# Mixers: the weights' sums and lower halves all on POOL, VectorE without them

## The chip, the cores and the metric

The kernel runs on one core of a Trainium2 chip. The metric is the device time of one execution in microseconds (us). The engines are PE (TensorE), DVE (VectorE), ACT (ScalarE), POOL (GpSimd) and SP, which here issues nearly all DMAs. Each engine works through its own list of instructions in order; the lists are fixed when the kernel is built, and engines wait for one another by semaphores.

## What is computed

One layer of an encoder, for 1,024 prompt tokens and 64 tokens of a running stream: a SwiGLU half step, then differential softmax attention and retention side by side (the mixers), merged by sigmoid gates, then a second SwiGLU half step and a norm. All in float32. The mixers begin with one wide projection:

```python
hm = modulate(rms_norm(x, norm_mix), shm, scm)
q_a, k_a, v_a, q_r, k_r, v_r, z_r, gate_a, gate_r = jnp.split(hm @ w_in, offsets, axis=-1)   # 1024 x 5120
o_a = diff_attention_prompt(q_a, k_a, v_a, lam)      # 4 heads, and one over a cache of 2048 for the stream
o_r, s_new = retention_prompt(q_r, k_r, v_r, log_g)  # 4 heads, states carried over blocks
```

## The kernel before

Three stages follow one another: the first SwiGLU, the mixers, then the merge and the second SwiGLU. The tokens are worked on in two groups, g = 0 (512 tokens) and g = 1 (576). The change concerns the mixers alone, where the wide projection of `w_in` is done 128 columns by 128.

**Split products.** A float32 factor is split into an upper half `hi` (a rounded copy, made by ACT, line 134) and a lower half `lo = x - hi` (line 138, on an engine that is handed in). `mm3` (lines 162 to 164) multiplies hi by hi, hi by lo and lo by hi, so each product of a 128-row slice is three matmuls, and the third needs the weights' lower half.

**Pairs.** Two blocks of 128 columns make a pair. `pair_weights` loads both (512 KB each, tiles `raw`: a1, a2 and b1, b2 are their halves) and forms Strassen-like sums (line 521): s1 = b1 + b2, s2 = s1 - a1, s3 = a1 - b1, s4 = a2 - s2. Four tiles are split: `ra` itself (call its halves wa), the tile of s1 and s2 (ws), the tile of s3 and s4 (wt), and b2 (wb, half as wide). `products` then makes 7 products of 12 matmuls from them, in this order: wa, ws, ws, wa, wt, wt, wb. In the mixers the tile of s1 and s2 is a slot called `h15` and that of s3 and s4 is `h14`. There are 20 pairs for each group, 40 in all; the weights of the first are made in the stage before, so 39 are made in the mixers.

**Buffers.** `whi` and `wlo` have 3 buffers each, so wa, ws and wt of a pair take the place of wa, ws and wt of the pair before, and each may be written only when its last product there has been done. `wb` has one buffer: it is free after the last product of the pair before.

**Who does what** is set by two lists for each stage. `LOE` names the engine for the lower halves of wa, ws, wt, wb and, fifth, of the down weights (not used in the mixers); `SE` names the engine for s1, s2, s3, s4. `phase(1)` puts the second row of `LOES` and `SES` in force for the mixers. `V` is `nc.vector` (DVE), `G` is `nc.gpsimd` (POOL).

**Around it.** Between the products, generators put in the attention (scores line 1067, row maximum 1071, exponential 1073, its coefficient 1079 and difference 1080 on DVE, values 1090), the rotation of retention (1207 to 1209, DVE), its norm (874 on DVE, then a power on POOL, 875), and the sums of the second group's activations (383 to 416, mostly DVE, one in four sums on POOL). DVE also reads every product out of PSUM and adds it up (line 521, `t`, `ft` and `u` with `misc` as an input, 128x256 or 128x288). When the group changes, the split activations of the next group are written (line 138, `h<-u,h`): five of seven on DVE, two on POOL. A scheduler with a timeline of its own sets the final order of each engine's list when the kernel is built, so a change of engines also moves instructions that it does not touch.

Of the kernel before, what the change touches and what calls it, by code (L numbers as in the profile page):

```python
# [83 lines left out]
def encoder_layer(tc: tile.TileContext, a, o, stage=9):  # L84
# [80 lines left out]

    V, G = nc.vector, nc.gpsimd
    LOE, SE = [], []
    LOES = [[G, V, V, V, G], [G, V, G, V, V], [G, V, V, G, G]]
    SES = [[G, G, G, G], [G, V, G, G], [V, V, G, G]]
    FE = [[V, V, G, G], [G, G, G, G], [V, V, V, G], [V, V, G, G]]  # L170

    def phase(i):
        LOE[:], SE[:] = LOES[i], SES[i]

# [1397 lines left out]
```

## Time and profile before

| | us |
|---|---|
| median of 3 runs | 2621.68 (2621.64 to 2623.53) |
| the profiled execution | 2621.47 |
| its span in the trace | 2619.7 |
| busy in the span: PE, DVE, POOL, ACT | 2479.6, 1992.8, 1621.9, 1079.0 |

The pairs made in the mixers start their first product at 883.8 us of the span, and the last pair's last product ends at 1606.6. In the trace matmuls are pipelined. A row of a group gives busy time, mean time of one, and the idle time of the engine ahead of it with what ended it. "Granted clock" 1.00 is 2.4 GHz, 0.50 is 1.2 GHz.

### The profile page before, as it was taken

What the parts mean: (1) busy time and instruction counts of PE and PEld (TensorE: products, weight loads), DVE (VectorE), ACT (ScalarE), POOL (GpSimd) and SP (SyncE); (2) the same over time, 40 slices, a digit from 0 to 9 for tenths busy, and PEclk for the clock granted to TensorE, in tenths of its full rate; (3) what the DMA queues carried; (4) which work ended last, traced back from release to release, by engine and by line L of the source; (5) the groups of instructions that cost most, each with busy time, mean ns of one, the idle gap of its engine ahead of it and who ended that gap; (6) DMA issues with size and microseconds to landing.
All of it is one profiled execution on the core that took longest, in us unless ns stands there. A gap on an engine that the chain in (4) does not pass through costs nothing. (4 is left out here: it accounts for less than half of the span.)

```text
span 2619.7 us, 45289 instructions
## 1 busy us (share of the span) xinstructions
PE 2479.6 (95%) x17278; PEld 2273.4 (87%) x17278; DVE 1992.8 (76%) x3241; ACT 1079.0 (41%) x1726; POOL 1621.9 (62%) x970
## 2 busy tenths in 40 slices
PE   6999999999999689998999999999999999999998
PEld 3888888999999678887888887798889998999998
DVE  6797778887767888788765675646898888877776
ACT  4443334443333333444434444533444435333333
POOL 4797677787665546667454543554777665766562
PEclk9999999999999899998999999999899999999999
DMA  8755446444443553444333335745443335323221
GB/s 276 222 181 161 150 141 209 144 151 137 152 133 107 180 173 111 155 134 131 109 101 106 118 103 160 232 138 182 149 152 117 105 106 180 104 89 97 90 87 40
DMA packets 427309, 367.60 MB, mean 140 GB/s; under 512 B 20060, under 2 KB 359700, under 8 KB 427092
## 3 DMA queue, kind: packets, MB, share of 16 engines
q1 hardware_dynamic: 426912, 364.65, 44.7%
q8 instruction: 136, 2.23, 0.3%
q14 instruction: 81, 0.66, 0.1%
q10 hardware_dynamic: 180, 0.06, 0.0%
HBM read 310.31 MB, written 52.10 MB: 138 GB/s over the span
## 5 line engine op out<-in xcount | busy, mean ns | idle before, releaser
L162 PE MATMUL misc<-h,whi 128*128 128x288 f32 (+2 forms) x3360 | 1012.2, 302 | 40.5 <-DVE t L521 21.9
L164 PE MATMUL misc<-h,wlo 128*128 128x288 f32 (+2 forms) x3360 | 986.2, 295 | 12.5 <-DVE wlo L138 11.5
L163 PE MATMUL misc<-h,whi 128*128 128x288 f32 (+2 forms) x3360 | 989.6, 295 | 5.0 <-DVE h L138 5.0
L162 PEld LDWEIGHTS misc<-h,whi 128*128 128x128 f32 x3360 | 645.5, 192 | 91.7 <-DVE t L521 25.1
L164 PEld LDWEIGHTS misc<-h,wlo 128*128 128x128 f32 x3360 | 644.8, 192 | 21.5 <-DVE wlo L138 13.5
L163 PEld LDWEIGHTS misc<-h,whi 128*128 128x128 f32 x3360 | 646.1, 192 | 13.9 <-DVE h L138 6.6
L138 POOL TENSOR_TENSOR wlo<-raw,whi 128x1024 fp32r<-128x1024 f32 x150 | 374.4, 2496 | 215.7 <-ACT whi L134 191.6
L521 DVE TENSOR_TENSOR t<-misc,t 128x256 f32<-128x256 f32 (+1 forms) x736 | 307.5, 432 | 252.8 <-PE misc L164 223.5
L138 DVE TENSOR_TENSOR wlo<-ws,whi 128x1024 fp32r<-128x1024 f32 x178 | 327.2, 1839 | 70.7 <-ACT whi L134 70.7
L138 POOL TENSOR_TENSOR wd<-raw,wd 128x1024 fp32r<-128x1024 f32 x88 | 210.8, 2415 | 142.1 <-ACT wd L134 142.1
L521 POOL TENSOR_TENSOR ws<-raw 128x512 f32<-128x512 f32 x134 | 194.2, 1452 | 117.8 <-DVE wlo L138 75.9
L643 DVE SCALAR_TENSOR_TENSOR x<-misc,gate,x 128x64 f32<-128x64 f32 (+3 forms) x540 | 237.1, 484 | 20.1 <-PE misc L164 19.4
L134 ACT CAST whi<-ws 128x1024 fp32r<-128x1024 f32 x178 | 186.5, 1048 | 159.6 <-PE misc L163 94.4
L134 ACT CAST whi<-raw 128x1024 fp32r<-128x1024 f32 x160 | 167.4, 1046 | 196.4 <-PE misc L163 157.3
L521 DVE TENSOR_TENSOR v<-t 128x288 f32<-128x288 f32 (+1 forms) x176 | 184.6, 1060 | 2.5 <-ACT t L604 2.3
L162 PE MATMUL misc<-h,wd 128*128 128x288 f32 (+3 forms) x552 | 178.1, 329 | 2.4 <-DVE t L521 1.6
L163 PE MATMUL misc<-h,wd 128*128 128x288 f32 (+3 forms) x552 | 179.8, 326 | 0.0
L164 PE MATMUL misc<-h,wd 128*128 128x288 f32 (+3 forms) x552 | 178.5, 326 | 0.0
L521 POOL TENSOR_TENSOR h<-raw 128x512 f32<-128x512 f32 x78 | 111.3, 1427 | 86.0 <-issue 39.1
L134 ACT CAST wd<-raw 128x1024 fp32r<-128x1024 f32 x88 | 88.3, 1047 | 170.4 <-PE misc L163 150.8
L162 PE MATMUL misc<-h,wb 128*128 128x256 f32 (+1 forms) x512 | 151.6, 296 | 1.9 <-ACT t L588 1.7
L163 PE MATMUL misc<-h,wb 128*128 128x256 f32 (+1 forms) x512 | 149.0, 291 | 0.0
(294 smaller groups left out, 4911.2 us busy)
## 6 DMA issues: line engine op xcount, KB each, us to landing
raw<-in_w_up_dram SPq DMA_DIRECT2D x176, 512.0 KB, 4.0
raw<-in_w_down_dram SPq DMA_DIRECT2D x88, 512.0 KB, 3.5
raw<-in_w_in_dram SPq DMA_DIRECT2D x80, 512.0 KB, 4.0
rawa<-in_w_ada_dram SPq DMA_DIRECT2D x88, 256.0 KB, 4.3
yf<-xsp SPq DMA_DIRECT2D x32, 288.0 KB, 4.2
h<-in_w_ada_dram SPq DMA_DIRECT2D x16, 512.0 KB, 6.8
raw<-in_w_o_dram SPq DMA_DIRECT2D x16, 512.0 KB, 4.7
raw<-far SPq DMA_DIRECT2D x14, 576.0 KB, 3.8
```

Source lines behind the costliest of these rows:

```text
L134: nc.scalar.copy(hi, src)
L138: eng.tensor_tensor(out=lo, in0=src, in1=hi.bitcast(F32), op=ALU.subtract)
L162: nc.tensor.matmul(out, wh, xh, start=first, stop=False)
L163: nc.tensor.matmul(out, wh, xl, start=False, stop=False)
L164: nc.tensor.matmul(out, wl, xh, start=False, stop=last)
L521: eng.tensor_tensor(out=out, in0=in0, in1=in1, op=op)
L643: nc.vector.scalar_tensor_tensor(out=xm, in0=t[:, c0 - cs.start:c1 - cs.start], scalar=gate()[:, m, s:s + 1], in1=xm, op0=ALU.mult, op1=AL ...
```

## The change

Two rows of the tables are other ones. In the mixers s2, the lower half of ws and the lower half of wb go from DVE to POOL, which then makes all four sums and all four lower halves of every pair.

```diff
-    LOES = [[G, V, V, V, G], [G, V, G, V, V], [G, V, V, G, G]]
-    SES = [[G, G, G, G], [G, V, G, G], [V, V, G, G]]
+    LOES = [[G, V, V, V, G], [G, G, G, G, V], [G, V, V, G, G]]
+    SES = [[G, G, G, G], [G, G, G, G], [V, V, G, G]]
```

Over the 39 pairs this moves 117 instructions from DVE's list to POOL's. What it does to the lists is shown where the first group's pairs are closest together (near 1180 us of the span). POOL before, from s1 of a pair (weights raw_13677 and raw_13678) to the lower half of its wt, with two instructions of its neighbours in between; h15 and h14 are the sums' tiles, raw the loaded weights, in brackets what an instruction waits for:

```order
L521 TENSOR_TENSOR h15_13681<-raw_13678 128x512 [waits DMAHW2_49,DVE_49,Pool_49]
L138 TENSOR_TENSOR wlo_13556<-h14_13542,whi_13555 128x1024 [waits PE_49,Activation_49]
L521 TENSOR_TENSOR h14_13682<-raw_13677,raw_13678 128x512 [waits DMAHW5_49,Pool_49]
L521 TENSOR_TENSOR h14_13682<-raw_13677,h15_13681 128x512 [waits DVE_49]
L138 TENSOR_TENSOR wlo_13684<-raw_13677,whi_13683 128x1024 [waits PE_49,Activation_49]
L521 TENSOR_TENSOR h15_13887<-raw_13884 128x512 [waits DMAHW7_49,DVE_49,Pool_49]
L138 TENSOR_TENSOR wlo_13696<-h14_13682,whi_13695 128x1024 [waits PE_49,Activation_49]
```

POOL now, for the same pair:

```order
L521 TENSOR_TENSOR h15_13681<-raw_13678 128x512 [waits DMAHW1_49,Pool_49]
L138 TENSOR_TENSOR wlo_13684<-raw_13677,whi_13683 128x1024 [waits DMAHW2_49,PE_49,Activation_49]
L521 TENSOR_TENSOR h14_13682<-raw_13677,raw_13678 128x512 [waits Pool_49]
L521 TENSOR_TENSOR h15_13681<-h15_13681,raw_13677 128x512 [waits Pool_49]
L138 TENSOR_TENSOR wb_13700<-raw_13678,wb_13699 128x512 [waits PE_49,Activation_49]
L521 TENSOR_TENSOR h14_13682<-raw_13677,h15_13681 128x512 [waits Pool_49]
L138 TENSOR_TENSOR wlo_13690<-h15_13681,whi_13689 128x1024 [waits Activation_49]
L138 TENSOR_TENSOR wlo_13696<-h14_13682,whi_13695 128x1024 [waits PE_49,Activation_49]
```

The lower half of ws (wlo_13690) now stands last but one of the eight, behind the one of wb, which waits for the last product of the pair before. DVE before, in the same pair:

```order
L521 TENSOR_TENSOR h15_13681<-h15_13681,raw_13677 128x512 [waits DMAHW5_49,Pool_49]
L521 TENSOR_TENSOR ft_13385<-misc_13519,t_13413 128x256 [waits DVE_49,PE_49]
L138 TENSOR_TENSOR wb_13560<-raw_13538,wb_13559 128x512 [waits DMAHW4_49,Activation_49]
L521 TENSOR_TENSOR t_13564<-misc_13580,t_13563 128x256 [waits DVE_49,PE_49,Activation_49]
L521 TENSOR_TENSOR t_13565<-misc_13594,t_13564 128x256 [waits DVE_49,PE_49]
L521 TENSOR_TENSOR ft_13535<-misc_13616,t_13563 128x256 [waits DMAHW1_49,PE_49]
L138 TENSOR_TENSOR wlo_13690<-h15_13681,whi_13689 128x1024 [waits Activation_49]
```

DVE now, at the same products:

```order
L521 TENSOR_TENSOR ft_13385<-misc_13519,t_13413 128x256 [waits DVE_49]
L521 TENSOR_TENSOR ft_13384<-misc_13500,t_13414 128x256 [waits PE_49]
L521 TENSOR_TENSOR ft_13535<-misc_13616,t_13563 128x256 [waits DMAHW0_49,PE_49,Activation_49]
L521 TENSOR_TENSOR t_13564<-misc_13580,t_13563 128x256 [waits DVE_49,PE_49]
L521 TENSOR_TENSOR t_13565<-misc_13594,t_13564 128x256 [waits DVE_49,PE_49]
```

Only the readings of products out of PSUM are left. PE's list moves with it; now, at the second and third product of such a pair (misc_13580 and misc_13594, weights ws):

```order
L162 MATMUL misc_13580<-h2_9708,whi_13549 128x256 [waits DVE_49,Activation_49]
L163 MATMUL misc_13580<-h3_9709,whi_13549 128x256
L162 MATMUL misc_13594<-h4_9716,whi_13549 128x256 [waits DVE_49]
L163 MATMUL misc_13594<-h5_9717,whi_13549 128x256
L1047 MATMUL misc_13609<-ident_66,rows_13133 128x128 [waits DVE_49]
```

Before, all 24 matmuls of the two products stood there in one run; now only the four that need no lower half do, and the others stand behind the fourth product and the first matmuls of the fifth and sixth.

## Rows read from the trace of the kernel before

**Rows 1.** The page's first part: busy us of each engine, share, instructions.

```profile
PE 2479.6 (95%) x17278; PEld 2273.4 (87%) x17278; DVE 1992.8 (76%) x3241; ACT 1079.0 (41%) x1726; POOL 1621.9 (62%) x970
```

**Rows 2.** Windows of the mixers: length, PE, PEld, DVE, ACT, POOL busy; granted clock; DMA.

```profile
883.80:1013.80 130.00, 101.82 (x673) 89.88 (x672) 109.00 (x215) 49.33 (x96) 69.60 (x47) 0.87 0.51 152
1013.80:1060.70 46.90, 46.90 (x348) 40.63 (x346) 37.66 (x89) 23.01 (x50) 33.29 (x20) 1.00 0.35 107
1060.70:1196.90 136.20, 131.34 (x995) 120.19 (x995) 113.41 (x202) 64.79 (x129) 95.25 (x57) 0.99 0.49 156
1196.90:1235.90 39.00, 28.91 (x183) 27.34 (x182) 32.48 (x40) 12.98 (x22) 25.12 (x14) 0.82 0.38 116
1235.90:1606.60 370.70, 365.92 (x2472) 311.98 (x2470) 251.61 (x481) 155.96 (x282) 177.02 (x117) 1.00 0.35 105
```

**Rows 3.** Groups of DVE in the mixers (883.8 to 1606.6), shapes apart.

```profile
L138 DVE TENSOR_TENSOR wlo<-h,whi 128x1024 fp32r<-128x1024 f32 x39 | 54.9, 1408 | 9.3 <-ACT whi L134 9.3
L521 DVE TENSOR_TENSOR h<-h,raw 128x512 f32<-128x512 f32 x38 | 53.7, 1412 | 5.6 <-POOL h L521 5.3
L138 DVE TENSOR_TENSOR wb<-raw,wb 128x512 fp32r<-128x512 f32 x39 | 45.9, 1177 | 3.1 <-ACT wb L134 2.4
```

**Rows 4.** Sums and lower halves in the mixers: ns min/median/max, first and last start.

```profile
L521 POOL TENSOR_TENSOR h<-raw x76: 1257/1300/2424, 887.5 to 1563.1; 128x512 f32<-128x512 f32 x76
...
L138 POOL TENSOR_TENSOR wlo<-h,whi x39: 2352/2397/2912, 888.7 to 1582.8; 128x1024 fp32r<-128x1024 f32 x39
L521 DVE TENSOR_TENSOR h<-h,raw x38: 657/693/2889, 891.5 to 1558.6; 128x512 f32<-128x512 f32 x38
```

**Rows 5.** The lower half of wb on POOL, in the second SwiGLU (same columns).

```profile
L138 POOL TENSOR_TENSOR wb<-raw,wb x44: 1262/1759/2270, 1830.0 to 2570.5; 128x512 fp32r<-128x512 f32 x44
```

**Rows 6.** Order of time, 895 to 920: start, us, engine, operation, [idle before].

```profile
896.03 0.28 PE L163 MATMUL misc<-h,whi 128*128 128x256 f32 x1
...
896.15 0.28 PE L164 MATMUL misc<-h,wlo 128*128 128x256 f32 x1
...
905.06 2.86 POOL L138 TENSOR_TENSOR wlo<-h,whi 128x1024 fp32r<-128x1024 f32 x1
...
906.09 1.84 DVE L1079 SCALAR_TENSOR_TENSOR col<-col,lam 128x1 f32<-128x1 f32 x1
...
908.56 0.73 DVE L388 TENSOR_TENSOR sqf<-sqf,yf 128x576 f32<-128x576 f32 x1
...
910.29 1.64 PE L1067 MATMUL S<-u 64*128 64x384 f32 x2 [6.73 <-ACT c L1073]
```

**Rows 7.** Groups of DVE, 883.8 to 1013.8.

```profile
L388 DVE TENSOR_TENSOR sqf<-sqf,yf 128x576 f32<-128x576 f32 x7 | 11.9, 1693 | 2.2 <-ACT yf L386 2.1
L521 DVE TENSOR_TENSOR h<-h,raw 128x512 f32<-128x512 f32 x7 | 9.8, 1402 | 0.5 <-POOL h L521 0.3
...
L138 DVE TENSOR_TENSOR wlo<-h,whi 128x1024 fp32r<-128x1024 f32 x7 | 8.5, 1216 | 1.6 <-ACT whi L134 1.6
...
L138 DVE TENSOR_TENSOR wb<-raw,wb 128x512 fp32r<-128x512 f32 x6 | 5.9, 991 | 0.0
```

**Rows 8.** Groups of POOL, 1060.7 to 1196.9, shapes apart.

```profile
L521 POOL TENSOR_TENSOR h<-raw 128x512 f32<-128x512 f32 x19 | 27.0, 1419 | 13.5 <-DVE wlo L138 2.7 <-PE misc L163 2.5 <-PE misc L164 2.4
L138 POOL TENSOR_TENSOR wlo<-raw,whi 128x1024 fp32r<-128x1024 f32 x10 | 24.8, 2476 | 15.8 <-ACT whi L134 15.8
L138 POOL TENSOR_TENSOR wlo<-h,whi 128x1024 fp32r<-128x1024 f32 x9 | 22.7, 2524 | 0.9 <-ACT whi L134 0.9
L521 POOL TENSOR_TENSOR h<-raw,h 128x512 f32<-128x512 f32 x10 | 15.2, 1521 | 0.6 <-DVE h L521 0.6
```

**Rows 9.** Waits of POOL, 1060.7 to 1196.9.

```profile
POOL col L875 <- DVE col L874: 9.9, 3, 4.8
```

**Rows 10.** A stretch of the first SwiGLU, columns as in the second group.

```profile
150.00:200.00 50.00, 48.74 (x354) 43.89 (x352) 44.98 (x56) 21.62 (x33) 46.13 (x28) 1.00 0.61 195
```

**Rows 11.** Groups of DVE at the change of group, 1196.9 to 1235.9.

```profile
L138 DVE TENSOR_TENSOR h<-u,h 128x576 fp32r<-128x576 f32 x7 | 13.2, 1913 | 0.0
```

## The prediction

> **What bounds the kernel now.** The page's first part comes first: PE is busy for 95% of the span and DVE for 76%, POOL for 62% [rows 1]. The change touches only the mixers, so the windows of the mixers come next, cut at the starts of pairs [rows 2]; in each the reader compares the stretch's length with PE, DVE and POOL.
>
> - 883.8 to 1013.8 (130.0 us, 6 pairs): PE busy 101.8, so idle 28.2, at a mean granted clock of 0.87. DVE is the fullest of the feeders at 109.0, POOL has 69.6.
> - 1013.8 to 1196.9 (46.9 + 136.2 = 183.1 us, 13 pairs): PE busy 178.2, clock near 1.00. DVE 151.1, POOL 128.5. Here PE bounds and neither feeder does.
> - 1196.9 to 1235.9 (39.0 us, the change of group): PE idle 10.1; DVE 32.5, POOL 25.1.
> - 1235.9 to 1606.6 (370.7 us): PE idle 4.8. POOL 177.0. PE bounds.
>
> So PE is idle for 38 us in the first and third of these stretches, and for 10 in the other 554. The longest single wait in the first is 6.73 us, on an exponential of the attention, and the order of time shows what was late behind it: DVE, which at 906.09 needs 1.84 us for a 128x1 operation that begins inside a 2.86 us lower half on POOL and ends with it [rows 6].
>
> That is a pattern. DVE's operations with two inputs in SBUF stretch when POOL runs: s2 takes 657 ns at best, 2889 at worst [rows 4], and its mean in the mixers is 1412 [rows 3].
>
> **What the change removes from DVE.** In the mixers the three kinds of moved instruction cost DVE 54.9 + 53.7 + 45.9 = 154.5 us [rows 3] over 39 pairs, 4.0 a pair (the first s2 starts ahead of the window).
>
> **What it adds to POOL.** A sum takes 1.30 us, a lower half of 128x1024 2.40 (medians, [rows 4]). The half-width lower half doesn't occur on POOL in the mixers; in the second SwiGLU it takes 1.26 at its shortest and 1.76 in the median [rows 5]. I take 1.3, near the shortest, since the DVE work that stretched it is what leaves. So 1.30 + 2.40 + 1.30 = 5.0 us a pair. A pair's own POOL work becomes 4 x 1.30 + 3 x 2.40 + 1.30 = 13.7 us, where its 84 matmuls, one every 0.12 us at full clock [rows 6], take 10, and the 13 pairs of the dense stretch follow one another at 183.1 / 13 = 14.1.
>
> Stretch by stretch, against the profiled execution's own time of 2621.47 us (span 2619.7 and 1.8 around it; the median of the runs is 0.2 above).
>
> *Dense stretch, 183.1 us.* POOL: 128.5 + 13 x 5.0 = 193.5. Its present instructions get shorter when DVE's rivals go: 19 x (1.419 - 1.30) + 10 x (1.521 - 1.30) + 10 x (2.476 - 2.40) + 9 x (2.524 - 2.40) = 6.3 us over 10 pairs [rows 8], so 8.2 over 13. That leaves 185.3 us in 183.1: POOL would have to work without a pause. It can't. It still waits for DVE's column ahead of the power of the norms (9.9 us over 10 pairs now, [rows 9]), and each lower half waits for a buffer that PE frees. With the fullest window that I read, 46.13 of 50 us or 92% [rows 10], the stretch needs 185.3 / 0.92 = 201.4, which is 18 more; without any pause it needs 2 more. I take +13, nearer the upper end: 185.3 plus the 9.9 us of that wait, and a microsecond for the buffers, is 196. What is queued behind: in the new order the lower half of ws stands behind that of wb, which waits for the last product of the pair before. After that product come 0.6 (the cast) + 1.3 + 1.3 (s4) + 2.4 = 5.6 us until ws is there, while PE has the rest of the fifth and sixth products (22 x 0.12), the first of the next (12) and the fourth (12) to do, 46 x 0.12 = 5.5. That fits alone, but leaves no room for a POOL that is already behind.
>
> *Start, 130.0 us.* DVE loses 9.8 + 8.5 + 5.9 = 24.2 us [rows 7]. POOL rises from 69.6 by 6 x 5.0 to about 100, from 54% to 77% of the stretch, so DVE's other operations with two SBUF inputs meet it more often: the 7 squares' sums average 1.69 us here [rows 7] where one takes 0.73 at its shortest [rows 6], so 6.7 us of theirs is waiting, and I estimate 10 more for the rotation and the far sums. If these 17 us grow as POOL's share does (77/54), 7 come back. Net DVE relief is 17 us. How much of it was on PE's path? PE is idle for 28.2 of 130 us, but the other 102 are PE's own, a part at the lower clock. I take half, -8. Bounds: 0, and -24 (all of it, without new contention).
>
> *Change of group, 39.0 us.* DVE loses 2 x 4.0 = 8 us and keeps 13.2 of activations that must be split [rows 11]. POOL rises from 25.1 by 2 x 5.0 to 35 of 39, and starts with what it is behind from the dense stretch. I take +3, between -6 (DVE was the late one) and +9 (POOL is late by its 10 new us, less one).
>
> *Rest, 370.7 us.* POOL 177.0 + 18 x 5.0 = 267, 72%: it has room, PE is the bound and can give back at most its 4.8 idle us. 0, from -3 to +5.
>
> *Everything else* stays: both SwiGLU stages and the merge use other rows of the tables, and what comes ahead of the mixers keeps its order. DMA count and sizes are the same.
>
> Sum: -8 + 13 + 3 + 0 = +8, so 2621.5 + 8 = **2629.5 us**.
>
> **A page that speaks against the change.** DVE's small operation was held to the end of POOL's [rows 6]. The Trainium skill, "Perfetto Trace Analysis", section "Optimizing Scalar/DVE Operations", says that GpSimd and VectorE share an SBUF read port, so that offloading between those two might not help. By that rule alone the result is rival B. And the Trainium skill, "SBUF — State Buffer", section "Who interferes with whom", says that a VectorE instruction with at most one SBUF input doesn't contend with GpSimd: by that the PSUM readings left in DVE's list run freely and rival C gains. The trace so far agrees with the second on the two-input operations.
>
> **Rivals.**
>
> A (the forecast): POOL becomes the bound where pairs are dense. For it: 185 us of work in 183. Against it: lower halves are made some microseconds ahead of need, so that a short excess is swallowed.
>
> B: it evens out. Start -11, dense +9, change of group +2, rest 0: 2621.5. For it: the terms are of one size and opposite sign.
>
> C: DVE's relief decides, faster. The place is the start: the full net relief of 17 us reaches PE, and 1 more come back through the clock, since short waits there go with 0.87. Dense +4, since POOL's 185 us run with next to no pause once DVE's column comes early, and the change of group -4. That is -18: 2603.5. It decides when POOL keeps busy for 99% of the dense stretch (185.3 in 183.1 + 4); at the 95% that +13 stands for, A wins.
>
> D: the change doesn't do what it says. The new lists show all 117 instructions on POOL, so I give it nothing.
>
> **How the numbers follow.** What a measurement of this kernel can tell from no change is about 0.2%, 5.2 us, so "same" is 2616.4 to 2626.9. A has 0.50, B 0.22, C 0.28. A's own range is 2627 to 2648 (start 0, dense 18, change of group 9 gives 2648.5). The range leaves out a little of C's far end and of A's: 2606 to 2648.
>
> **What would show it.** A: in the 13 dense pairs POOL's share above 90%, and PE with new waits on a lower half from POOL (line 164, weights ws). C: PE's idle time of the first 6 pairs under 14 us, DVE there under 95 busy, clock above 0.92. Contention: the two-input operations that stay on DVE (1079, 1080, 1207, 388) get longer, not shorter, while POOL's sums fall to about 1.3 us. I am wrong if the dense stretch doesn't get longer than 187 us, or if PE waits for POOL after 1236 us too.

## The result, and the profile after

The changed kernel takes 2640.31 us (median; 2635.75 to 2641.66), the kernel before 2621.66: a ratio of 1.0075, 95% interval 1.0057 to 1.0092. It is slower by 18.6 us. Direction and range hold; the predicted 2629.5 is 10.8 us short, so that the rise is more than twice the 8 us forecast. All figures below are of fast runs: one of the five runs of e2_but_one took 3407.58 us at a mean granted clock of 0.65 and is left out. The profiled execution after took 2635.75 us (span 2633.9), 14.3 more than the profiled one before.

The page's first part of the kernel after, to be laid beside [rows 1]:

```profile
PE 2483.1 (94%) x17278; PEld 2276.9 (86%) x17278; DVE 1883.1 (71%) x3124; ACT 1079.3 (41%) x1726; POOL 1800.7 (68%) x1087
```

DVE has 117 instructions and 110 us fewer, POOL 117 more and 179 us more, PE 3.5 us more. The windows of the mixers, cut at the starts of the same pairs as in [rows 2] (columns: length; busy us of PE, PEld, DVE, ACT, POOL; granted clock; share of the DMA engines; GB/s):

```profile
890.30:1023.00 132.70, 102.72 (x674) 91.47 (x674) 100.11 (x198) 50.18 (x99) 100.58 (x65) 0.86 0.50 151
1023.00:1069.10 46.10, 46.10 (x347) 40.31 (x346) 28.04 (x77) 22.00 (x48) 42.38 (x28) 1.00 0.38 114
1069.10:1215.30 146.20, 134.44 (x993) 122.97 (x992) 79.70 (x176) 64.25 (x129) 136.76 (x85) 0.96 0.47 145
1215.30:1255.80 40.50, 30.55 (x187) 27.77 (x187) 23.09 (x36) 13.95 (x23) 39.49 (x25) 0.87 0.33 99
1255.80:1628.50 372.70, 364.91 (x2473) 312.15 (x2473) 211.42 (x426) 155.38 (x281) 260.96 (x171) 0.99 0.35 106
```

The start is 2.7 us longer than before, the dense pairs 46.1 + 146.2 = 192.3 against 183.1, the change of group 1.5 longer. In the dense pairs POOL is busy for 42.38 + 136.76 = 179.1 us, 93%, where it was 70%; DVE fell from 151 to 108 there. Of TensorE's waits from 880 to 1650 us these stand out (engine, tile, line, what it waited for: us in all, times, longest):

```profile
PE misc L162 <- ACT whi L134: 14.8, 7, 6.7
PE misc L162 <- DVE t L521: 12.3, 6, 5.2
PE misc L1282 <- DVE s L1272: 8.4, 3, 6.7
```

The first is new: the cast on ACT ends the wait. What was late behind the cast differs by place. In the change of group (9.0 us of the 14.8, most of it in two waits of 6.75 and 2.02) it is POOL: each of the two casts had itself waited 5.17 us for one of POOL's sums. The first of them, in order of time on POOL, ACT and PE (start, us, engine, operation, [idle before and what ended it]):

```profile
1220.82 1.77 POOL L521 TENSOR_TENSOR h<-h,raw 128x512 f32<-128x512 f32 x1
...
1222.63 1.04 ACT L134 CAST whi<-h 128x1024 fp32r<-128x1024 f32 x1 [5.17 <-POOL h L521]
...
1223.72 0.61 PE L162 MATMUL misc<-h,whi 128*128 128x288 f32 x1 [6.75 <-ACT whi L134]
```

In the dense pairs (four waits, 5.8 us, all in the last three pairs) POOL's sum was ready 1.4 to 5.4 us before the cast began. There the cast stood in ACT's list behind other work that waits for PE, three times behind the copy of the same pair's first product out of PSUM (line 895):

```profile
1186.96 1.30 POOL L521 TENSOR_TENSOR h<-h,raw 128x512 f32<-128x512 f32 x1
...
1189.67 0.37 ACT L895 COPY t<-misc 128x256 f32<-128x256 f32 x1 [3.33 <-PE misc L164]
...
1189.94 1.05 ACT L134 CAST whi<-h 128x1024 fp32r<-128x1024 f32 x1
...
1191.04 0.39 PE L162 MATMUL misc<-h,whi 128*128 128x256 f32 x1 [1.45 <-ACT whi L134]
```

In the kernel before, the cast of a dense pair's sum tile begins 5.9 to 12.4 us ahead of that copy. After, it is 1.5 to 9.6 us ahead of it in the first ten dense pairs, where four casts start as soon as POOL's sum ends, and 0.3 to 1.4 us behind it in the last three. The time goes the same way: the copies are 8.8 us later than in the kernel before at the first dense pair (1024.3 against 1015.5) and 7.1 at the tenth (1157.1 against 1150.0). So the stretch's loss is made in its last pairs, when the lead is used up.

The longest wait of PE in the dense pairs, 4.05 us, is of another kind. A read-out of PSUM by DVE (`ft`) stood behind line 1080, which took 2.80 us beside POOL's lower halves; the mean of that shape was 0.96 us before:

```profile
1158.02 4.71 POOL L138 TENSOR_TENSOR wlo<-h,whi 128x1024 fp32r<-128x1024 f32 x2
...
1160.48 2.80 DVE L1080 SCALAR_TENSOR_TENSOR c<-c,col,c 128x512 f32<-128x512 f32 x1
...
1163.76 0.55 PE L162 MATMUL misc<-h,whi 128*128 128x256 f32 x1 [4.05 <-DVE ft L521]
```

The kinds of instruction of [rows 3] are gone from DVE; they stand on POOL now, with its own, where these are the largest groups (mixers; busy us, mean ns of one, idle before):

```profile
L138 POOL TENSOR_TENSOR wlo<-h,whi 128x1024 fp32r<-128x1024 f32 x78 | 189.7, 2436 | 48.4 <-ACT whi L134 45.2 <-PE misc L1150 2.0 <-PE misc L164 1.0
L521 POOL TENSOR_TENSOR h<-raw 128x512 f32<-128x512 f32 x76 | 105.2, 1391 | 0.9
...
L138 POOL TENSOR_TENSOR wb<-raw,wb 128x512 fp32r<-128x512 f32 x39 | 51.7, 1326 | 12.8 <-ACT wb L134 12.7
L521 POOL TENSOR_TENSOR h<-h,raw 128x512 f32<-128x512 f32 x38 | 51.4, 1353 | 0.9
```

### The profile page after: what moved, and what is told of

It is laid out like the page before. It is cut to its first block, busy times and chain, and to the rows that moved or that the text cites. A ratio compares the mean times of both kernels' runs of the same rounds, so it can differ in the third digit from the quotient of the medians.

```text
span 2633.9 us, 45291 instructions
## 1 busy us (share of the span) xinstructions
PE 2483.1 (94%) x17278; PEld 2276.9 (86%) x17278; DVE 1883.1 (71%) x3124; ACT 1079.3 (41%) x1726; POOL 1800.7 (68%) x1087
## 5 line engine op out<-in xcount | busy, mean ns | idle before, releaser
L164 PE MATMUL misc<-h,wlo 128*128 128x288 f32 (+2 forms) x3360 | 985.8, 296 | 11.3 <-DVE wlo L138 10.3
L138 POOL TENSOR_TENSOR wlo<-h,whi 128x1024 fp32r<-128x1024 f32 x78 | 189.7, 2436 | 48.4 <-ACT whi L134 45.2
L138 POOL TENSOR_TENSOR wb<-raw,wb 128x512 fp32r<-128x512 f32 x83 | 126.7, 1527 | 124.1 <-ACT wb L134 117.8
L162 PE MATMUL misc<-h,wb 128*128 128x256 f32 (+1 forms) x512 | 151.2, 295 | 3.5 <-ACT t L588 1.7
```

Of the source, the lines that this page charges most:

```text
L138: eng.tensor_tensor(out=lo, in0=src, in1=hi.bitcast(F32), op=ALU.subtract)
L162: nc.tensor.matmul(out, wh, xh, start=first, stop=False)
L164: nc.tensor.matmul(out, wl, xh, start=False, stop=last)
```

## The experiments

In the texts of this section the left tile is `ra` (halves wa), the sum tile that of s1 and s2 (ws), the right tile b2 (wb). The table is made from all experiments. It gives the median against that of the kernel before on the same chip, then from the profile the lengths of the four stretches (cut at the first matmuls of the same pairs; the last one reaches to the merge's first pair, 1628.7 in the kernel before, and so is longer than that of [rows 2]; cuts here and above differ by up to 0.4 us), and POOL's busy us and share in the dense pairs.

```
kernel            us against before   start  dense  change   rest   POOL in the dense pairs
before                                130.0  183.1   39.0   392.8   128.6  70%
after                 +18.6           132.6  192.4   40.5   392.8   179.2  93%
e1_first               +3.1           134.6  180.4   39.1   392.8   128.7  71%
e2_but_one            +16.4           130.0  195.1   38.2   394.1   177.4  91%
e3_dense              +11.0           129.3  194.0   36.5   393.8   177.4  91%
e4_late                -4.3           128.9  182.3   38.4   391.4   127.6  70%
e5_ws                 +12.4           134.2  184.5   39.4   399.0   154.7  84%
e6_s2_wb              -16.3           125.1  178.8   38.9   388.1   149.4  84%
e7_relief             -20.2           122.1  176.0   30.2   392.5   120.0  68%
e8_load               +68.9           148.9  209.7   45.9   410.3   194.0  93%
e9_s2                  -0.4           128.6  178.2   37.1   404.1   138.0  77%
e10_wb                -13.9           125.3  179.8   40.5   389.1   140.0  78%
e11_swap               -0.6           131.3  179.1   35.7   398.1   159.4  89%
e12_relief_ws         -24.5           124.1  172.0   37.5   386.5   126.8  74%
```

Where a stretch has the tables of before (start in e3 and e4, dense and rest in e1), its length comes back within 3 us, mostly within about 1. Each length is of one profile. At the pair that starts at 814.6 in the kernel before, ahead of the change, the others already stand 0.3 to 6.9 us later (after: 6.9), and that is in no term.

### By place: e1_first, e3_dense, e4_late

The changed tables become a fourth row of both tables, taken by some of the pairs only (here the first seven, of which the very first has its weights from the stage before; 7 to 19 in e3_dense, from 20 on in e4_late):

```diff
-    SES = [[G, G, G, G], [G, V, G, G], [V, V, G, G]]
+    SES = [[G, G, G, G], [G, V, G, G], [V, V, G, G], [G, G, G, G]]
...
+        count[0] += 1
+        phase(3 if count[0] <= 6 else 1)
         ws = early_w.pop((ma, mb), None) or pair_weights(...)
```

> The changed tables are used only for the first seven pairs of the mixers, the tables of before for all others. VectorE's order has the second rotation multiply (L1207) ahead of the first retention normalisation (L1272), as in the changed kernel. Theory 1 (three separate costs: the turned order in the start, GpSimd full in the dense pairs, little elsewhere): the first four intervals gain about 5 us, the turned order gives back 8.4 us, the dense pairs take their 183 us of before, so the time is 2622 to 2628 us (+3). Theory 2 (all of the loss is GpSimd's extra work in the dense pairs): a gain of some 5 us is kept, 2614 to 2618. Theory 3 (the loss comes with the extra GpSimd work wherever it stands, 0.47 us a pair): 2625.

> The changed tables are used only for the 13 dense pairs in the middle of the mixers (the pairs that end the first group), the tables of before for all others. Theory 1 (GpSimd is the bound in the dense pairs): they take 190 to 195 us instead of 183, GpSimd is busy over 92% of them, and the time is 2629 to 2632 us. Theory 2 (the loss there is only what the start's disturbance leaves behind): they take 183 to 186 us, and the time is 2620 to 2625.

> The changed tables are used only from the change of group on (the last 20 pairs of the mixers), the tables of before until then. Theory 1 (the last pairs wait for TensorE, and GpSimd has room): the change of group is 0 to 3 us longer and the rest 0 to 3 us, so 2621 to 2627 us. Theory 3 (0.47 us a pair, wherever the extra GpSimd work stands): 2631. Theory 4 (VectorE's relief is worth something there): under 2619.

e1 took 2623.03 us, ratio 1.0012 (1.0002 to 1.0022). e3 took 2630.91, 1.0041 (1.0029 to 1.0053). e4 took 2615.67, 0.9985 (0.9972 to 0.9997). e1 and e3 came as theory 1 has it, with 194.0 us in e3's dense pairs (POOL 91% busy, where it had set over 92%); theory 2 of each falls. Theory 3 (0.47 us a pair) gives e1's number as well, +3.3 for the seven pairs, and falls with e4, +9.4 against -4.3. e4 gained, by theory 4's number, but its profile has only 0.6 + 1.4 us of that in the stretches whose tables differ. The dense pairs are where most of the loss is made. The three parts sum to +9.8, the whole is +18.6. That what one stretch leaves on POOL can be worked off by the next under the old tables (e1: start +4.6, dense -2.7) and not under the new ones would fit this; no run tests it.

### The turned order: e2_but_one

In the kernel after, DVE's list has the second rotation ahead of the first retention normalisation (L1272), which was the other way about before. Two views in order of time, of DVE and of PE, show what that does at 984 (start, us, engine, operation, [idle before and what ended it]):

```profile
987.51 1.04 DVE L1207 TENSOR_TENSOR u<-u,rt 128x256 f32<-128x256 f32 x1 [4.11 <-DMA rt<-u]
...
990.54 0.72 DVE L1272 TENSOR_SCALAR s<-S,mv,col 128x128 f32<-128x128 f32 x2
```

```profile
991.08 0.45 PE L1282 MATMUL misc<-ident,s 128*128 128x128 f32 x1 [6.72 <-DVE s L1272]
```

DVE stands 4.11 us for the rotation's DMA while the normalisation behind it is ready, and PE stands 6.72 us. The copy of the pair's first product (line 895) comes 9.6 us later than in the kernel before at the pair behind the stall (1001.1 against 991.5), and came 0.9 later at the pair ahead of it (975.2 against 974.3). The edit gives one pair the old tables, which turns the order back there:

```diff
+        count[0] += 1
+        phase(3 if count[0] != 5 else 1)
```

> The change in full, but for one pair (the sixth of the mixers' start), which keeps the tables of before; with that, VectorE's order has the first retention normalisation (L1272) ahead of the second rotation multiply (L1207) again, as before the change. Theory 1 (the turned order costs 8.4 us by itself): the idle time of 6.7 us of TensorE on L1272 is gone and the time is 2630 to 2634 us. Theory 2 (the jump of 8.4 us is GpSimd's backlog, and the order only shows where it is met): TensorE waits as long for another product of GpSimd there, and the time stays at 2638 to 2642.

It took 2636.3 us, 1.0060 (1.0047 to 1.0073): 16.4 above the kernel before on its chip, where the kernel after is 18.6 above. The wait on L1282 is gone, but at the next block PE waits about as long for the same line of DVE, there ahead of L1246 (both two lines lower in this file; waits of PE in the start):

```profile
PE S L1248 <- DVE s L1274: 6.0, 1, 6.0
```

The start is 2.6 us shorter than in the kernel after and the dense pairs 2.7 longer. So theory 2 is nearer, though the time lies between the two: the order settles where the stall is met, and little of the sum; the intervals of the two kernels overlap. PE's waits for this normalisation also go with the start's length in the other runs. In the starts that got longer than before (after, e1, e5, e8, e11) they sum to 5.8 to 9.6 us, in the others to at most 3.9, but for e2's 6.0 in a start of the old length. That is a concurrence and no test.

### By instruction: e5_ws, e6_s2_wb, e9_s2, e10_wb

e5 has one of the moved instructions, e6 the other two, e9 and e10 one of those each (the tables' second rows):

```diff
 before     LOES [G, V, G, V, V]   SES [G, V, G, G]
+e5_ws      LOES [G, G, G, V, V]   SES [G, V, G, G]
+e6_s2_wb   LOES [G, V, G, G, V]   SES [G, G, G, G]
+e9_s2      LOES [G, V, G, V, V]   SES [G, G, G, G]
+e10_wb     LOES [G, V, G, G, V]   SES [G, V, G, G]
```

> One part of the change alone: in all pairs of the mixers only the lower half of the sum tile (128 x 1024, 2.4 us on GpSimd) goes from VectorE to GpSimd; s2 and the lower half of the right tile stay on VectorE. GpSimd gets about 2.4 us a pair and stays near 155 us of work in the 183 us of the dense pairs. Theory 1 (the loss is a bound by GpSimd's total: it costs only once GpSimd is full): no loss in the dense pairs, 2616 to 2623 us. Theory 2 (each lower half that comes later off GpSimd costs a piece of its own, in proportion): half of the change's loss, 2628 to 2631 us.

> The other two parts of the change alone: s2 and the lower half of the right tile (128 x 512 each, 1.3 us each on GpSimd) go to GpSimd in all pairs of the mixers, the lower half of the sum tile stays on VectorE. GpSimd gets about 2.6 us a pair and stays near 155 us of work in the 183 us of the dense pairs. Theory 1 (a bound by GpSimd's total): 2616 to 2623 us. Theory 2 (in proportion): 2628 to 2631 us; with e5_ws the two losses then add up to that of the whole change, some 19 us.

> One part of the change alone: only s2 goes to GpSimd in the mixers' pairs (1.3 us there, 1.41 us off VectorE). s4 on GpSimd reads s2 and the cast of the sum tile needs it, so two changes of engine go with it. Theory 1 (what decides is how long the moved instruction takes on each engine: s2 and the lower half of the right tile cost VectorE as long as GpSimd, the sum tile's lower half costs GpSimd 2.4 us for 1.4 us): half of the gain of e6_s2_wb, 2609 to 2615 us. Theory 2 (all of that gain is the change of engine that s2 no longer needs): 2602 to 2607. Theory 3 (it is all the right tile's): 2617 to 2623.

> One part of the change alone: only the lower half of the right tile goes to GpSimd in the mixers' pairs (1.3 us there, 1.18 us off VectorE); s2 and the sum tile's lower half stay on VectorE. Theory 1 (by the time on each engine): 2609 to 2615 us, as e9_s2. Theory 2 (all of the gain of e6_s2_wb is the change of engine that s2 no longer needs): 2617 to 2623. Theory 3 (it is all the right tile's): 2602 to 2607.

e5: 2632.69 us, 1.0045 (1.0032 to 1.0059). e6: 2603.99, 0.9939 (0.9926 to 0.9951), faster than both kernels and than both of its theories. e9: 2620.17, 0.9991 (0.9978 to 1.0003). e10: 2606.68, 0.9949 (0.9934 to 0.9965). Two thirds of the change are a gain of 16 us; the sum tile's lower half turns it into a loss of 19. Proportion falls with that: +12.4 and -16.3 don't add up to +18.6. By their times e9 and e10 both come out as theory 3 has it: nearly all of the gain is the right tile's, and the time on each engine (theory 1) doesn't foretell e9's zero. In the dense pairs theory 1 holds, since at 84% of POOL neither e5 nor e6 loses more than 1.4 us there (dense pairs of e5, then of e6):

```profile
1017.80:1202.30 184.50, 179.28 (x1338) 161.45 (x1338) 143.48 (x284) 84.89 (x172) 154.72 (x87) 0.99 0.46 142
```

```profile
1011.70:1190.50 178.80, 177.05 (x1339) 159.42 (x1338) 127.12 (x268) 84.90 (x173) 149.42 (x98) 1.00 0.45 143
```

Its number for e5 misses; theory 2's 2628 to 2631 us is nearer, but the dense pairs have only 1.4 of the 12.4. With nearly the same load on POOL, DVE is relieved by 24 us in e6 and by 7.6 in e5, where 13 instructions of 1.41 us [rows 3] should give 18. DVE's groups in the mixers of e5 show one place where that went: the half-width lower half that stays on DVE takes 1404 ns instead of 1177.

```profile
L138 DVE TENSOR_TENSOR wb<-raw,wb 128x512 fp32r<-128x512 f32 x39 | 54.8, 1404 | 5.1 <-ACT wb L134 4.4
```

e5's loss is in its start and its rest, and e9's (+11.3 in the rest) cancels what it gained before. e5's start has the stall on the normalisation (PE S L1246, 7.2 us in one wait). For e9's rest the pauses of PE and the windows show it, first those of e9:

```profile
1253.04 1.84 PE L1155 MATMUL misc<-ck,s 128*128 128x512 f32 x2 [2.91 <-DVE ck L1152]
...
1271.23 0.61 PE L162 MATMUL misc<-h,whi 128*128 128x288 f32 x1 [3.17 <-DVE ft L521]
```

```profile
1250.00:1260.00 10.00, 7.09 (x39) 5.95 (x38) 5.30 (x8) 2.39 (x5) 3.44 (x3) 0.83 0.32 93
1260.00:1270.00 10.00, 7.37 (x52) 6.45 (x50) 6.68 (x10) 2.58 (x3) 6.56 (x5) 1.00 0.42 118
1270.00:1280.00 10.00, 8.77 (x23) 5.77 (x24) 8.79 (x17) 4.21 (x10) 1.94 (x2) 0.52 0.34 103
1280.00:1290.00 10.00, 10.00 (x35) 6.05 (x34) 0.93 (x3) 1.04 (x2) 0.00 (x0) 0.63 0.21 55
```

Then those of before at the same work:

```profile
1266.59 0.40 PE L162 MATMUL misc<-h,whi 128*128 128x288 f32 x1 [3.92 <-DVE t L521]
```

```profile
1255.00:1265.00 10.00, 6.80 (x42) 5.31 (x41) 6.56 (x10) 2.68 (x5) 4.21 (x3) 1.00 0.29 82
1265.00:1275.00 10.00, 8.41 (x49) 7.94 (x50) 6.62 (x14) 2.65 (x3) 1.74 (x2) 0.83 0.49 139
1275.00:1285.00 10.00, 10.00 (x63) 8.11 (x62) 8.29 (x16) 5.00 (x12) 5.35 (x3) 1.00 0.34 97
```

Before, PE pauses once for long and the granted clock falls to 0.83. In e9 it pauses twice for about 3 us (2.91 and 3.17), and then the grant is 0.52 and 0.63 for 20 us, near the lower level of 1.2 GHz. In e9's rest PE is idle 4.0 us more than before and busy 7.3 more (390.6 against 383.3) with the same 2588 matmuls. So some four of the 11.3 us are waiting, and some seven go with the lower clock. Which turn in the lists brings the second pause isn't settled; nor is what lengthens the rest of e5.

### Relief and load apart: e7_relief, e8_load, e12_relief_ws

e7 puts copies on ACT in place of all three moved instructions, e12 in place of the sum tile's lower half alone, so both leave out the differences themselves and only their time counts; e8 leaves DVE as before and has POOL do three of its own instructions twice.

```diff
 e7, e12
+    def half(src, hi, lo, eng):
...
+        nc.scalar.copy(hi, src)
+        nc.scalar.copy(lo, src)
...
-        split(s12, *ws, LOE[1])
+        half(s12, *ws, LOE[1])
 e7 alone
-        add(s2, s1, a1, ALU.subtract, SE[1])
+        nc.scalar.copy(s2, s1) if LOE[4] is V else add(s2, s1, a1, ALU.subtract, SE[1])
-        split(b2, *wb, LOE[3])
+        half(b2, *wb, LOE[3])
 e8
         add(s1, b1, b2, ALU.add, SE[0])
+        if LOE[4] is V:
+            add(s1, b1, b2, ALU.add, SE[0])
```

(In e8 s3 and the lower half of the left tile are doubled in the same way. `LOE[4] is V` holds in the mixers alone.)

> VectorE's relief without GpSimd's load: the three moved instructions are replaced by copies on ScalarE in the mixers, so s2 and two of the lower halves are not the real differences there. VectorE has 3 instructions fewer a pair, GpSimd is as before, ScalarE has 3 more. Theory 1 (VectorE does not bound the dense pairs, but the start and the change of group wait for it a little): 2609 to 2618 us. Theory 2 (VectorE's relief is worth nothing anywhere): 2618 to 2623. Theory 3 (it is worth much, and GpSimd's load hides that): under 2605.

> GpSimd's load without VectorE's relief: VectorE does all that it did before, and GpSimd makes s1, s3 and the lower half of the first tile twice in the mixers' pairs, which is 5.0 us a pair more, as much as the change adds to it. Theory 1 (GpSimd's total bounds the dense pairs, and VectorE's relief gives a little back elsewhere): 2640 to 2655 us, the loss again in the dense pairs. Theory 2 (the loss of the change comes from which halves are late and not from GpSimd's total): under 2630.

> VectorE is relieved of the sum tile's lower half alone, and GpSimd is not loaded: a copy on ScalarE takes its place in the mixers' pairs, so that lower half is not the real difference there. Everything else is as before. Against e5_ws, which has the same instruction on GpSimd, it tells what GpSimd's 2.4 us a pair cost. Theory 1 (the relief is worth its part of e7_relief's 20 us, and the load on GpSimd turns it into a loss): 2608 to 2616 us, so the load costs 17 to 25 us. Theory 2 (this instruction is worth nothing on VectorE): 2617 to 2623, and the load costs some 12 us. Theory 3 (e5_ws loses by the order into which the change puts the work, whichever engine does it): over 2625.

e7: 2600.08 us, 0.9922 (0.9906 to 0.9937). e8: 2689.12, 1.0259 (1.0239 to 1.0279). e12: 2594.16, 0.9912 (0.9892 to 0.9932). Taken off DVE and not put on POOL, the work is worth 20 us or more, so in e7 theory 3 has the number, and in e12 the gain lies beyond theory 1's own. The load alone costs 69, far above theory 1's number. e5 and e12 lie 12.4 + 24.5 = 37 us apart, with the one lower half on POOL in e5 and a copy on ACT in e12; the copy doesn't wait for its cast, so this is no clean price either. The dense pairs of e7 and e8:

```profile
1006.10:1182.10 176.00, 176.00 (x1339) 159.29 (x1338) 92.94 (x254) 111.48 (x212) 120.00 (x76) 1.00 0.49 150
```

```profile
1035.20:1244.90 209.70, 185.01 (x1319) 163.73 (x1318) 169.48 (x290) 83.45 (x172) 194.01 (x111) 0.97 0.39 121
```

With DVE relieved PE works there without a pause. With POOL loaded, POOL is 93% busy again: its 194.0 us of work take 209.7, as the 179.2 of the kernel after take 192.4. At the 92% of [rows 10] they would take 210.9 and 194.8. In e8 DVE's own instructions stretch too; its lower half of the sum tile, 1408 ns in [rows 3], is the row to see (DVE's groups in the mixers):

```profile
L138 DVE TENSOR_TENSOR wlo<-h,whi 128x1024 fp32r<-128x1024 f32 x39 | 76.1, 1950 | 8.3 <-ACT whi L134 8.3
```

So a part of the 69 us is DVE's, and e8 is no clean price of POOL. Nor are e7 and e12 of DVE's relief alone, since ACT does more in them. That e12, which relieves less, is no slower than e7 isn't explained.

### Another tile on POOL: e11_swap

```diff
-    LOES = [[G, V, V, V, G], [G, G, G, G, V], [G, V, V, G, G]]
+    LOES = [[G, V, V, V, G], [V, G, G, G, V], [G, V, V, G, G]]
```

> The change in full, but VectorE makes the lower half of the left tile (128 x 1024) in the mixers' pairs in place of that of the sum tile. GpSimd and VectorE have just as much to do as in e6_s2_wb, and 2.4 us a pair less on GpSimd than with the change. Theory 1 (the sum of GpSimd's work decides: the change loses only because GpSimd is over 90% busy in the dense pairs): 2600 to 2610 us, as e6_s2_wb; the dense pairs take 177 to 181 us and GpSimd is under 86% busy in them. Theory 2 (the sum tile's lower half is bad on GpSimd by its place, since it holds the next sums back): 2625 us or more.

It took 2620.06 us, 0.9996 (0.9984 to 1.0008): no change, between the two theories. Against the kernel after it is some 19 us better, with 2.4 us a pair less on POOL. The dense pairs take what theory 1 says, 179.1 us, though POOL is 89% busy where it had set under 86%:

```profile
1017.60:1196.70 179.10, 172.51 (x1339) 157.62 (x1338) 124.27 (x265) 89.01 (x179) 159.42 (x100) 1.00 0.47 147
```

The start (+1.3) and the rest (+5.3) take back what the dense pairs and the change of group gain (7.3), so POOL's sum is not all that decides there. The table's last column now has a step in it: up to 89% of POOL the dense pairs take 172 to 185 us, from 91% on 192 to 210. A share is known only afterwards; in work, which can be added up before, the step lies between 159 us of POOL's and 177.

## Why the prediction was right, and where its sum was wrong

- **What bounds.** Right for the dense pairs by the experiments: the loss comes and goes with POOL's work there (e3, e8, e11), and POOL is 93% busy, close to the 92% that was read from [rows 10]. Rival A's sign, over 90%, came true. Its other sign did not: the waits were forecast on the lower half (line 164) and stand on the cast (line 162). Only in the change of group is a late sum of POOL's seen to end them. In the dense pairs POOL uses up the lead of the casts, as the argument against A had it for a short excess; the waits at the end are then made by the order of ACT's list and by one stretched instruction of DVE. That the builder's own timeline put the casts late because POOL is full is likely and not shown. Of the signs of being wrong neither came: the dense stretch takes 192 us, more than 187, and after 1256 us (1236 before) PE has no wait for POOL or for a cast.
- **Dense, +13: measured +9.3.** Of it 6.9 us are idle time of PE (11.8 against 4.9) and 2.4 are busy time at a lower clock. POOL's work was sized at 185.3 us and was 179.2. The 9.9 us of waiting for DVE's column [rows 9], which the forecast kept, is gone in 1069.1 to 1215.3; what POOL waits for there is almost all the cast:

```profile
POOL wlo L138 <- ACT whi L134: 7.1, 7, 2.8
POOL wb L138 <- ACT wb L134: 1.1, 1, 1.1
```

- **Start, -8: measured +2.6.** This is the term that failed; as like stretches differ by up to 3 us, it shows that the start got no shorter. The step that failed is that POOL's new load was costed there as contention on DVE alone (7 us), with no term for a wait that the load or the new order of the lists brings to PE. The relief did come at first: the stretch begins 6.2 us later than in the kernel before, and at the pair ahead of the stall the lag is 0.9. The stall then takes all of it back and more (9.6 behind it). e1, with the whole change in the start and nowhere else, lengthens it by 4.6 us. POOL was 76% busy over the stretch, close to the 77% forecast; it works in bursts there, stands still while its order waits (9.15 us ahead of wb at 999), and DVE's list puts the normalisation behind a rotation that waits for a DMA. The parts of that, 10 us in all, aren't priced singly; e2 shows only that turning the order back at one place moves the stall. That e7, without POOL's load, is 7.9 us shorter in the start agrees with -8 in part by luck: the -8 was half of a relief from which the contention had been taken off, and in e7 ACT does more.
- **Change of group, +3: +1.5. Rest, 0: 0.0** to the merge's first pair (392.8 both). Both within their bounds. The first is the small difference of large parts: PE waits 9.0 us for casts there, and e7, without POOL's load, is 8.8 us shorter. The second could have come otherwise: parts of the change alone give -4.7 (e6) to +11.3 (e9) in the rest.
- **Everything else, 0.** The mixers account for 2.6 + 9.3 + 1.5 = 13.4 us of the 14.3 between the two profiled executions; 6.2 us that the profile after has ahead of the mixers and about 5 that it has less behind the merge's start are of the size that such stretches differ by from profile to profile (0.3 to 6.9 us at 814.6, as above; 983.0 to 991.1 us behind the merge's start). The profiled execution after is the fastest of its four, and what the other three took longer has no profile.
- **Rival B** (it evens out) is what e9 and e11 measured, not the change. **Rival C** rested on a real 20 us (e7, e12), but its condition, POOL at 99% in the dense pairs, was not met, and none of its signs in the start came: PE idle 30.0 us (under 14), DVE busy 100.1 (under 95), clock 0.86 (above 0.92).
- **Offloading as such.** The Trainium skill, "Perfetto Trace Analysis", section "Optimizing Scalar/DVE Operations", warns that moving work between GpSimd and VectorE might not help. e9 and e11 (no change), e5 and the change (losses) agree; e6 and e10 don't, they gain 0.6% and 0.5%.
- **Contention.** Of the four lines named, 1079 went from 533 to 700 ns and 1080 rose in most of its shapes, as forecast; 388 fell from 1693 to 1284 and 1207 (256 columns) from 1177 to 927, against it, while 1209 behind it rose from 412 to 1354. POOL's plain sums fell only from 1431 to 1391 in the mean.

## What to carry to other kernels

Before moving work to another engine, add up the receiver's work in the fullest stretch: here the dense pairs lost next to nothing with up to 159 us of POOL's work beside 172 to 179 of PE's (POOL 89% busy), and 9 us or more with 177 and up (91 to 93%). Move part of it: the two instructions that took both engines about as long (1.4 and 1.2 us on DVE, 1.3 on POOL) were a gain of 16 us together, the third (1.4 against 2.4) a loss of 12 alone. That the time on each engine is the reason isn't shown: of the two, s2 alone gained nothing and the right tile's lower half 14, and each choice of engines also turns the order of the lists, which no run here holds fixed. And an in-order engine that is 76% busy in the mean is not free at each moment; its load wants a price of its own there.

## What was not expected of the hardware

A DVE instruction with one small input in SBUF was held by POOL, on the path to the normalisation. In the kernel after, in order of time on DVE and then on POOL:

```profile
1069.28 2.21 DVE L874 TENSOR_SCALAR col<-mv 128x2 f32<-128x2 f32 x1
1071.40 0.28 DVE L1231 TENSOR_TENSOR s<-S,c_kdec 128x128 f32<-128x128 f32 x1
```

```profile
1069.07 2.40 POOL L138 TENSOR_TENSOR wlo<-h,whi 128x1024 fp32r<-128x1024 f32 x1
```

It begins inside POOL's lower half and ends with it, 2.21 us for two columns, where its shortest of this shape and the half-height one takes 0.16. Its mean went from 393 ns before to 713. The reciprocals beside it, one input as well, take 132 to 165 ns in all 32 cases:

```profile
L1078 DVE RECIPROCAL col<-col 128x1 f32<-128x1 f32 x32 | 5.0, 155 | 6.1 <-ACT c L1073 5.8
```

The prediction cited only that a VectorE instruction with one SBUF input doesn't contend. The same section of the Trainium skill ("SBUF — State Buffer", "Who interferes with whom") excepts the two-port modes, which it says tensor_scalar can enter. The rows agree with that exception and with the rule for the reciprocal; in which mode the instruction ran, no row shows.
